# Prompt attention of a hybrid decoder layer: scores by halves of the sequence and classes of positions modulo 4, other load times for cache tiles, a later store

## The chip, the cores and the metric

The kernel runs on one core of one Trainium2 chip. The metric is the time of one execution on the device in microseconds (us); a kernel's time is the median of its runs. The engines have short names: PE multiplies matrices, DVE and ACT work on vectors, POOL is a slower vector engine, SP issues most DMAs. Each runs its own instruction stream in order and waits for the others through semaphores.

## What is computed

One layer of a decoder for two groups of tokens with the same weights: a prompt of 256 positions, and a sample group of 8 sequences with 4 new positions each, whose past keys and values lie in caches. Cut to what matters:

```
z = x @ w_in                       # h, gate_b, gate_c, q, k, v, g_a, g_b
A = gate_b * conv3(gate_c * h)     # causal, width 3; its last rows are a state to return
B: groups (window, dilation) = (128,1), (512,4), (2048,16), 4 heads of 128 each:
   position t sees s = t - dil*i, i = 0..128; score q.k*scale - slope*(t-s)
   softmax over the keys of all three groups together, per head
x1 = LN(ALPHA*x + W_o[sigmoid(g_a)*(A W_a) + sigmoid(g_b)*(B W_b)])
y  = LN(ALPHA*x1 + (silu(conv3(a))*b) W_down),  [a, b] = x1 W_up
```

Also returned are the new keys and values, the caches moved on, and the last rows of both convolutions. All is float32. In group 0 a position sees the 128 positions before it. In group 1 it sees only positions that are equal to it modulo 4, and in group 2 modulo 16; in a prompt of 256 all of those back to the start lie in the window.

## The kernel before, in words

*Products.* Everything is held as features by tokens: 128 partitions of features, 288 columns of tokens (256 of the prompt, 32 of the sample), the even tokens ahead of the odd ones in most tiles. A product (`product`, L202) multiplies one block of 128 output features with all tokens: up to 16 blocks of 128 input features, each with three matmuls (L221, L222, L223), high part of the weight by high and low part of x, and low part of the weight by high part of x. ACT makes the high part of a weight block (`whi`) and DVE the low part (`wlo`) from the float32 load, both in `split` (L227), in two halves of 8 blocks. `prepare` (L177) issues the load of the next product's weights on SP (L182), 1 MB each, into one of three buffers `wst`; the halves of `whi` and `wlo` have four buffers each. The products come in this order: 12 for the queries, 24 for keys and values (head by head), 48 for mixer A, 32 for gate a beside W_a, 32 for gate b beside W_b, 16 for W_o, and the feed-forward part.

*Order.* A scheduler places the instructions on each engine when the kernel is built, from the order in which the code emits them and its own guess of times. `behind` (L139) ties a DMA to stand behind the last weight load. So the place of an instruction on its engine is fixed, and an engine whose next instruction waits does nothing else.

*Prompt attention* (`prompt_attention`, L344) is a generator for one head, advanced between products. First the scores: the queries of the even positions and those of the odd positions (`qb` 0 and 1), 128 each, against 256 keys in group 0 (L353) and against the 128 keys of the same parity in groups 1 and 2 (L355); distances `m_dist`, with 1e30 at keys that aren't seen, are multiplied and added on DVE (L364). Row maximum (L369), exponential on ACT (L371), and normalisation (L373) follow. Two products later PE transposes the values (L378) and the weights (L387), and ACT copies them to SBUF (L384, L391). One product later PE multiplies them (L395). These matmuls are float32, and each is two instructions on PE; a transpose is one.

*Distances* are loaded by `load_distances` (L328) with four DMAs, L336 and L337, after the fifth query product.

*The sample's part.* The caches of groups 0, 1 and 2 come as 18 key tiles (`in_ck`) and 18 value tiles (`in_cv`) of 1 MB, through three buffers `cache`. Tiles 0 and 1 belong to group 0 and are multiplied on PE (L472). Each other tile is multiplied elementwise, half on ACT (L437) and half on DVE (L441), and summed on DVE (L443). `sample_events` (L449) gives each step a place, counted in products: a key tile n at 13, 14, then 2.75 apart; value tiles at 64, 65, then 2.5 apart; its load (`cache_load`, L423, issued at L425) 5 products ahead (L551).

*The state of mixer A*, `cm`, is filled by POOL (L620, L621) and stored at L657, after the 48 products of mixer A.

*Copies* of the caches from input to output (L146) go on SP behind some of the weight loads from the 93rd on.

Of the kernel before, what the change touches and what calls it, by code (L numbers as in the profile page):

```python
# [35 lines left out]
NG, NH = 3, 4  # L36
DIL = (1, 4, 16)
BAND = 128
SCALE = P**-0.5
# [15 lines left out]
C_M0 = C_TM + NT  # L55
# [3 lines left out]
C_M1 = C_M0 + NG * P  # L59
# [17 lines left out]
SQ = 32  # L77
SCORES_AT = 13
TILE_K = 2.75
VALUES_AT = 64  # L80
TILE_V = 2.5

# [11 lines left out]
def layer_kernel(ctx: ExitStack, tc: tile.TileContext, ins, outs):  # L94
    nc = tc.nc
    pe, dve, act, pool, sp = nc.tensor, nc.vector, nc.scalar, nc.gpsimd, nc.sync
# [12 lines left out]
    def sb(pl, shape, tag, dt=F32, bufs=None):  # L109
        return pl.tile(shape, dt, tag=tag, name=nm(tag), bufs=bufs)  # L110
# [22 lines left out]
    w_load = [None]  # L133
    steps_on = [False]
    n_product = [2]
# [3 lines left out]
    def behind(i, after):  # L139

        tc.add_manual_dep(i.ins, after.ins.name, no_sync, reason="pace")
# [156 lines left out]

    pa = sb(big, [P, KD * T], "yal")

    m_dist = pa[:, : 2 * NG * SEQ].rearrange("p (h g k) -> p h g k", h=2, g=NG)
    pa_at = [2 * NG * SEQ]

    def pa_take(n):
        pa_at[0] += n
        return pa[:, pa_at[0] - n : pa_at[0]]

    v_two = [pa_take(2 * NG * P).rearrange("p (b g d) -> p b g d", b=2, g=NG) for _ in range(2)]
    s_two = [pa_take(MW) for _ in range(2)]
    xs_flat = xs.rearrange("p k t -> p (k t)")  # L310
    q_all = xs_flat[:, : NH * NG * T].rearrange("p (j g t) -> p j g t", j=NH, g=NG)
    sT_two = [xs_flat[:, NH * NG * T + c * MW : NH * NG * T + (c + 1) * MW] for c in range(2)]
    oT = pa_take(2 * P)
    prm = sb(big, [P, R_W], "prm")
    ident = cst[:, C_ID : C_ID + P]
# [9 lines left out]
    )  # L325
    v_s = sb(big, [P, NH, NG, NS], "v_s")

    def load_distances():  # L328

        pool.memset(m_dist[: P // 2, :, :, P:], BIG)  # L330
        m0, m1 = (
            ins["cst"][:, c : c + NG * n * P].rearrange("(a h) (g k) -> h a g k", h=2, g=NG)
            for n, c in ((1, C_M0), (2, C_M1))
        )
        for h in range(2):
            behind(sp.dma_start(m_dist[: P // 2, h, :, :P], m0[h]), w_load[0])  # L336
            behind(sp.dma_start(m_dist[P // 2 :, h], m1[h]), w_load[0])  # L337

    def in_a_row(row):

        for before, i in zip(row, row[1:]):
            behind(i, before)

    def prompt_attention(j, qT, kT, vT):  # L344


        q4 = h3(qT)[:, :, :, :P]
        k4, v4 = (t[:, :, :SEQ].rearrange("p g (a h) -> p g h a", h=2) for t in (kT, vT))
        s3 = [att(MW) for _ in range(2)]
        row = [last_mm[0]]  # L350
        for qb in range(2):
            row += [
                pe.matmul(s3[qb][:, : 2 * P], q4[:, 0, qb], kT[:, 0, :SEQ], start=True, stop=True)  # L353
            ] + [
                pe.matmul(s3[qb][:, (1 + g) * P : (2 + g) * P], q4[:, g, qb], k4[:, g, qb], start=True, stop=True)  # L355
                for g in range(1, NG)
            ]
        in_a_row(row)
        s = s_two
        for qb in range(2):  # L360
            for g in range(NG):
                c, n = (0, 2 * P) if g == 0 else ((1 + g) * P, P)
                m = m_dist[:, qb, g] if g == 0 else t2(m_dist[:, qb, g])[:, qb]
                dve.scalar_tensor_tensor(  # L364
                    s[qb][:, c : c + n], m, -SLOPE[g][j] / SCALE, s3[qb][:, c : c + n], ALU.mult, ALU.add
                )
        for qb in range(2):
            st = sb(wk, [P, 4], "st", bufs=4)
            dve.reduce_max(st[:, 0:1], s[qb], AX.X)  # L369
            dve.tensor_scalar_mul(st[:, 1:2], st[:, 0:1], -SCALE)  # L370
            act.activation(s[qb], s[qb], AF.Exp, bias=st[:, 1:2], scale=SCALE, accum_out=st[:, 2:3])  # L371
            dve.reciprocal(st[:, 3:4], st[:, 2:3])
            dve.tensor_scalar_mul(s[qb], s[qb], st[:, 3:4])  # L373
        yield 2
        v = v_two[j % 2]
        pv = [att(NG * P) for _ in range(2)]
        row = [last_mm[0]] + [
            pe.transpose(  # L378
                pv[kb][:, g * P : (g + 1) * P], vT[:, 0, kb * P : (kb + 1) * P] if g == 0 else v4[:, g, kb], ident
            )  # L380
            for kb in range(2) for g in range(NG)
        ]
        for kb in range(2):
            act.copy(v[:, kb], pv[kb].rearrange("p (g d) -> p g d", g=NG))  # L384
        pt = [sb(ps, [P, MW], "acc") for _ in range(2)]
        in_a_row(row + [
            pe.transpose(pt[qb][:, c * P : (c + 1) * P], s[qb][:, c * P : (c + 1) * P], ident)  # L387
            for qb in range(2) for c in range(MW // P)
        ])
# [4 lines left out]
        in_a_row([last_mm[0]] + [  # L394
            pe.matmul(  # L395
                po[:, qb * P : (qb + 1) * P], v[:, c if c < 2 else qb, max(0, c - 1)], sT_two[qb][:, c * P : (c + 1) * P],
                start=c == 0, stop=c == MW // P - 1,
            )
            for qb in range(2) for c in range(MW // P)
        ])  # L400
        act.copy(oT, po)
        split(h2(ybh[:, j])[:, :, :P], h2(ybl[:, j])[:, :, :P], oT.rearrange("p (h a) -> p h a", h=2))


# [44 lines left out]
    def sample_events():  # L449
# [121 lines left out]
    for j in range(NH):  # L571
        for g in range(NG):
            act.copy(h2(q_all[:, j, g]), q_first.pop(0) if q_first else product(x))
            if j == 1 and g == 1:
                load_distances()
            elif j == 1:
                for dst, src in ((prm, ins["prm"]),) if g else (
                    (cst[:, :C_BM], ins["cst"][:, :C_BM]),
                    (bmask, ins["cst"][:, C_MASK : C_MASK + MASK]),
                ):  # L580
                    behind(sp.dma_start(dst, src), w_load[0])
            steps_on[0] = j * NG + g >= 4
        pool.tensor_copy(q_s[:, :, j, :].rearrange("p g (a h) -> p g h a", h=2), h3(q_all[:, j])[:, :, :, P:])
    for j in range(NH):
        kT, vT = (kv[:, j % 2, c] for c in range(2))
        for g in range(NG):
            for t in (kT, vT):
                act.copy(t[:, g, :].rearrange("p (a h) -> p a h", h=2), product(x).rearrange("p h a -> p a h"))
        pool.tensor_copy(k_s[:, :, j, :], kT[:, :, SEQ:])
# [49 lines left out]
    for i in range(KD):  # L639
# [14 lines left out]
        ya = sb(wk, [P, T], "ya", bufs=2)  # L654
        gated(ya, y, pb)
        split(yah[:, i], yal[:, i], ya)
    sp.dma_start(outs["o_cm"].rearrange("p (k r) -> p k r", k=KD), cm)  # L657


    ma = dd_all.rearrange("p (k t) -> p k t", t=T)  # L660
    for i in range(KD):
        pg = product(x)
        sg = sb(wk, [P, T], "h", bufs=2)
        act.activation(h2(sg), pg, AF.Sigmoid)
        o = product((h3(yah), h3(yal)))
        dve.tensor_tensor(h2(ma[:, i]), h2(sg), o, ALU.mult)
    n_product[0] += 1000
    for _ in steps:
        pass
# [388 lines left out]
```

## Time and profile before

| | us |
|---|---|
| median of 3 runs (1736.32 to 1737.24) | 1736.93 |
| the profiled execution | 1737.77 |
| its span, first to last instruction | 1736.0 |
| PE busy | 1714.2 |
| DVE busy | 1103.5 |
| ACT busy | 869.6 |
| POOL busy | 244.3 |
| SP's wait for DVE's split at L182 | 1310.8 |

The mean granted clock of PE is 0.996. A row of the order of time has the start in us, the length in us, engine, line, operation, output <- inputs, shapes and a count of equal ones that follow each other; in square brackets stands how long the engine was idle before it and what ended that. A row of a table of stretches has the stretch, its length, then busy time and count of instructions of PE, PEld (weight loads), DVE, ACT and POOL, then the granted clock, the DMA engines' share and GB/s. A row of waits has who waited for whom, then the total in us, the number of waits and the longest.

### The profile page before, as it was taken

How to read it: one execution, taken by the hardware profiler on the slowest of the kernel's cores; microseconds unless marked ns; L12 is line 12 of the kernel's file. 1: busy time of each engine (PE TensorE's matmuls, PEld its weight loads, DVE VectorE, ACT ScalarE, POOL GpSimd, SP SyncE). 2: the span in 40 equal slices, each digit the busy share in tenths (PEclk: the TensorE clock that was granted, in tenths of full speed). 3: DMA queues.
4: the chain of work that ended last, by engine and by line, in shares of the span. 5: the costliest groups of instructions: out<-in, count | busy, mean ns of one | idle time of the engine just before them, and what ended most of it. 6: DMA issues, size and time to landing. Idle time of an engine off the chain costs nothing.

```text
span 1736.0 us, 33482 instructions
## 1 busy us (share of the span) xinstructions
PE 1714.2 (99%) x14034; PEld 1708.0 (98%) x14034; DVE 1103.5 (64%) x1406; ACT 869.6 (50%) x1398; POOL 244.3 (14%) x404
## 2 busy tenths in 40 slices
PE   9999999999999999999999999999999999999996
PEld 9999999999999999999999999999999999999996
DVE  5576667657775564455788888865555554555554
ACT  5465555545555443344445655544444443344444
POOL 0000000000000000010354333200111100011165
PEclk9999999999999999999999999999999999999998
DMA  9676565665666676687866667666676666776652
GB/s 338 241 281 221 226 249 216 225 243 216 254 235 242 277 304 244 237 310 299 301 261 244 250 256 271 249 261 243 255 279 245 258 250 248 263 266 255 238 205 95
DMA packets 57463, 436.14 MB, mean 251 GB/s; under 512 B 7456, under 2 KB 9504, under 8 KB 17440
## 3 DMA queue, kind: packets, MB, share of 16 engines
q1 hardware_dynamic: 55584, 429.29, 65.3%
q10 hardware_dynamic: 1728, 4.72, 0.7%
q8 instruction: 109, 1.79, 0.4%
q14 instruction: 42, 0.34, 0.1%
HBM read 427.53 MB, written 94.53 MB: 301 GB/s over the span
## 4 chain that ended last, share of the span: by engine, by line
PE 92%; DMA 4%; DVE 2%; ACT 1%; issue 1%; SPq 0%; ACTq 0%; DVEq 0%
PE acc L221 30%; PE acc L223 30%; PE acc L222 30%; DMA cache<-in_cv 3%; PE acc L289 1%; DVE wlo L227 1%; DMA cache<-in_ck 1%; DVE sw L443 1%; PE att L395 0%; DMA wst<-in_w_in 0%; ACT cache L437 0%; ACT whi L227 0%; ACT yah L784 0%; DVE dd L760 0%; PE att L472 0%
## 5 line engine op out<-in xcount | busy, mean ns | idle before, releaser
L227 DVE TENSOR_TENSOR wlo<-wst,whi 128x1024 fp32r<-128x1024 f32 (+2 forms) x584 | 704.1, 1209 | 450.0 <-ACT whi L227 448.1
L227 ACT CAST whi<-wst 128x1024 fp32r<-128x1024 f32 (+2 forms) x584 | 590.9, 1016 | 705.4 <-PE acc L222 628.9
L221 PE MATMUL acc<-xh,whi 128*128 128x288 f32 (+1 forms) x3216 | 921.7, 287 | 0.3 <-ACT whi L227 0.3
L222 PE MATMUL acc<-xl,whi 128*128 128x288 f32 (+1 forms) x3216 | 919.2, 286 | 0.0
L223 PE MATMUL acc<-xh,wlo 128*128 128x288 f32 (+1 forms) x3216 | 917.0, 285 | 1.9 <-DVE wlo L227 1.9
L223 PEld LDWEIGHTS acc<-xh,wlo 128*128 128x128 f32 x3216 | 605.1, 188 | 2.8 <-DVE wlo L227 2.8
L221 PEld LDWEIGHTS acc<-xh,whi 128*128 128x128 f32 x3216 | 605.1, 188 | 1.5 <-issue 1.0
L222 PEld LDWEIGHTS acc<-xl,whi 128*128 128x128 f32 x3216 | 606.4, 189 | 0.0
L223 PE MATMUL acc<-yah,wlo 128*128 128x288 f32 x1216 | 348.3, 286 | 2.0 <-DVE wlo L227 1.9
L221 PE MATMUL acc<-yah,whi 128*128 128x288 f32 x1216 | 347.7, 286 | 0.2 <-ACT whi L227 0.2
L222 PE MATMUL acc<-yal,whi 128*128 128x288 f32 x1216 | 347.7, 286 | 0.0
L223 PEld LDWEIGHTS acc<-yah,wlo 128*128 128x128 f32 x1216 | 229.8, 189 | 3.0 <-DVE wlo L227 3.0
L221 PEld LDWEIGHTS acc<-yah,whi 128*128 128x128 f32 x1216 | 229.7, 189 | 0.4 <-ACT whi L227 0.4
L222 PEld LDWEIGHTS acc<-yal,whi 128*128 128x128 f32 x1216 | 229.8, 189 | 0.0
L620 POOL COPY qk_s<-u 128x2 f32<-128x2 f32 x44 | 38.0, 864 | 571.9 <-ACT u L835 449.0
L443 DVE TRANSPOSE_TENSOR_REDUCE sw<-cache 128x32 f32<-128x1024 f32 x64 | 77.3, 1232 | 0.4 <-ACT cache L437 0.3
L608 DVE SCALAR_TENSOR_TENSOR cy<-u,prm,cy 128x304 f32<-128x304 f32 x120 | 74.9, 624 | 3.8 <-ACT cy L606 0.7
L437 ACT ACTIVATE cache<-cache,dd 128x128 f32<-128x128 f32 x128 | 39.3, 388 | 58.3 <-DMA cache<-in_cv 58.3
L680 POOL TENSOR_TENSOR ya<-ya,dd 128x288 f32<-128x288 f32 x16 | 13.6, 850 | 296.3 <-DVE ya L679 296.3
L441 DVE TENSOR_TENSOR cache<-cache,dd 128x512 f32<-128x512 f32 x32 | 20.8, 688 | 52.3 <-DMA cache<-in_cv 52.3
L437 ACT ACTIVATE cache<-cache,qk_s 128x128 f32<-128x128 f32 x128 | 39.6, 389 | 22.5 <-DMA cache<-in_ck 21.4
L227 ACT CAST yah<-ya 128x288 fp32r<-128x288 f32 x76 | 32.7, 430 | 24.7 <-DVE ya L631 8.5
(181 smaller groups left out, 901.7 us busy)
## 6 DMA issues: line engine op xcount, KB each, us to landing
wst<-in_w_in SPq DMA_DIRECT2D x113, 1024.0 KB, 4.9
wst<-in_w_up SPq DMA_DIRECT2D x88, 1024.0 KB, 4.9
wst<-in_w_down SPq DMA_DIRECT2D x32, 1024.0 KB, 4.9
cache<-in_ck SPq DMA_DIRECT2D x18, 1024.0 KB, 7.2
cache<-in_cv SPq DMA_DIRECT2D x18, 1024.0 KB, 8.0
wst<-in_w_a SPq DMA_DIRECT2D x16, 1024.0 KB, 5.9
wst<-in_w_out SPq DMA_DIRECT2D x16, 1024.0 KB, 4.9
wst<-in_w_down SPq DMA_DIRECT2D x16, 768.0 KB, 4.2
```

The lines of the kernel that those rows point to most:

```text
L221: pe.matmul(out, hi[:, c, :], xh_k, start=k == 0, stop=False)
L222: pe.matmul(out, hi[:, c, :], xl_k, start=False, stop=False)
L223: last_mm[0] = pe.matmul(out, lo[:, c, :], xh_k, start=False, stop=k == nk - 1)
L227: return act.copy(hi, src), dve.tensor_tensor(lo, src, f32(hi), ALU.subtract)
L289: i = pe.matmul(o[b], first_w(term == 2, b, k), xk, start=k == 0 and term == 0, stop=k == KD - 1 and term == 2)
L437: act.activation(e_t, e_t, AF.Copy, scale=w[:, g + 1, j, b * NT + t : b * NT + t + 1])
L441: dve.tensor_tensor(e3, e3, w3, ALU.mult)
L443: dve.tensor_reduce(parts[:, g, :, j, b * NT : (b + 1) * NT].rearrange("p k j t -> p j t k"), c[:, 2 * half * cols : (2 * half + 2) * cols ...
L608: dve.scalar_tensor_tensor(y, u[:, i : i + YW], prm[:, w0 + i : w0 + i + 1], y, ALU.mult, ALU.add)
L620: pool.tensor_copy(dst[:, 0:2], u[:, SEQ : SEQ + 2])
L680: pool.tensor_tensor(m, m, ma[:, i], ALU.add)
```

## The change

The diff, cut to its core:

```
-MW = (2 + NG - 1) * P
+NM = NG * P
+NC = 4
+LEAD = 7
...
-    def load_distances():
-        pool.memset(m_dist[: P // 2, :, :, P:], BIG)
-        for h in range(2):
-            behind(sp.dma_start(m_dist[: P // 2, h, :, :P], m0[h]), w_load[0])
-            behind(sp.dma_start(m_dist[P // 2 :, h], m1[h]), w_load[0])
+    def distances():
+        pool.memset(s_two[0][:, P + 2 * SQ :], 0.0)
+        for b, c0 in ((1, C_M1), (0, C_M0)):
+            for c in range(NC):
+                for dst, m in (...):
+                    behind(sp.dma_start(dst, m), w_load[0])
+                    yield
...
+        for g in range(1, NG):
+            pool.tensor_copy(v_cls..., vT[:, g, :SEQ].rearrange("p (b u c) -> p c b u", b=2, c=NC))
...
-        for qb in range(2):
-            pe.matmul(s3[qb][:, : 2 * P], q4[:, 0, qb], kT[:, 0, :SEQ], ...)
-            pe.matmul(s3[qb][:, (1 + g) * P : (2 + g) * P], q4[:, g, qb], k4[:, g, qb], ...)  # g = 1, 2
+        for b in range(2):
+            n = (b + 1) * P
+            pe.matmul(s3[b][:, :n], q_0[:, b], kT[:, 0, :n], ...)
+            for g in range(1, NG):
+                for r in range(2):
+                    for c in range(2):
+                        at = slice(SQ * (2 * r + c), SQ * (2 * r + c + 1))
+                        pe.matmul(by_class[at, g - 1], q5[:, g, b, r, c], k5[:, r, c, : b + 1, g - 1], ...)
...
-        for qb in range(2) for c in range(MW // P): pe.transpose(pt[qb]...)
+        for b in range(2) for c in range(b + 2):    pe.transpose(pt[b]...)
...
-        for qb in range(2) for c in range(MW // P): pe.matmul(po[:, qb * P : (qb + 1) * P], v[...], sT_two[qb]...)
+        pe.matmul(h2(po), v[:, 0], sT_old, start=True, stop=False)
+        pe.matmul(po[:, P:], v[:, 1], sT_two[1][:, P : 2 * P], ...)
+        for c in range(NC):
+            pe.matmul(h2(po)[:, :, at], v[:, 2 + 2 * (c % 2) + c // 2], sT_cls[:, :, at], ...)
...
-                yield at - 5, partial(cache_load, which, n)
+                yield at - LEAD, partial(cache_load, which, n)
...
-            if j == 1 and g == 1:
-                load_distances()
+            if n_product[0] > 4:
+                for _ in range(3):
+                    next(m_loads, None)
...
+        for b in range(2):
+            pool.tensor_copy(q_0[:, b]..., h3(q_all[:, j])[:, 0, :, b * P // 2 : (b + 1) * P // 2]...)
...
-    sp.dma_start(outs["o_cm"]..., cm)              # after the 48 products of mixer A
+        if i == 1:                                 # two steps into gate a
+            sp.dma_start(outs["o_cm"]..., cm)
```

The rows of scores are now the first and the second half of the positions (b = 0 and 1), each ordered by class modulo 4. In group 0 the first half is multiplied with 128 keys only and the second with all 256. In groups 1 and 2 each class of 32 queries is multiplied with the 32 or 64 keys of its own class up to its half; the four classes write to four quarters of the partitions. Rows of weights are 192 and 384 long (the first padded to 256 with zeros for the transposes) in place of 512 each. Before the products of a head POOL copies group 0's queries into that order, and after them the values of groups 1 and 2 by class. The distances come with 16 DMAs, three after each query block from the sixth on. Cache tiles' loads are emitted 7 products ahead in place of 5. The store of mixer A's state is emitted two steps, four products, later.

More of the change, by code (lines that the diff above doesn't have):

```diff
@@ L344, in prompt_attention @@
     def prompt_attention(j, qT, kT, vT):
-        q4 = h3(qT)[:, :, :, :P]
-        k4, v4 = (t[:, :, :SEQ].rearrange("p g (a h) -> p g h a", h=2) for t in (kT, vT))
-        s3 = [att(MW) for _ in range(2)]
-        row = [last_mm[0]]
-        for qb in range(2):
[L352 to L357, printed above, removed]
@@ L358, in prompt_attention @@
-        in_a_row(row)
[L359 to L367, printed above, removed]
+        q5 = h3(qT)[:, :, :, :P].rearrange("p g r (b u c) -> p g b r c u", b=2, c=2)
@@ new lines, in prompt_attention @@
+        k5 = kT[:, 1:, :SEQ].rearrange("p g (b u c r) -> p r c b g u", b=2, c=2, r=2)
+        for g in range(1, NG):
+            pool.tensor_copy(
+                v_cls.rearrange("p c (b g u) -> p g c b u", b=2, g=2)[:, g - 1],
+                vT[:, g, :SEQ].rearrange("p (b u c) -> p c b u", b=2, c=NC),
+            )
+        s3 = [att((b + 1) * P + (b + 1) * 2 * SQ) for b in range(2)]
+        row = [last_mm[0]]
+        for b in range(2):
+            n = (b + 1) * P
+            row.append(pe.matmul(s3[b][:, :n], q_0[:, b], kT[:, 0, :n], start=True, stop=True))
+            by_class = s3[b][:, n:].rearrange("p (b g u) -> p g b u", g=2, u=SQ)
+            for g in range(1, NG):
+                for r in range(2):
+                    for c in range(2):
+                        at = slice(SQ * (2 * r + c), SQ * (2 * r + c + 1))
+                        row.append(pe.matmul(
+                            by_class[at, g - 1], q5[:, g, b, r, c], k5[:, r, c, : b + 1, g - 1], start=True, stop=True
+                        ))
@@ new lines, in prompt_attention @@
+        in_a_row(row)
+        s = [s_two[b][:, : (b + 1) * (P + 2 * SQ)] for b in range(2)]
+        for b in range(2):
+            n = (b + 1) * P
+            dve.scalar_tensor_tensor(
+                s[b][:, :n], m_dist[b][:, :n], -SLOPE[0][j] / SCALE, s3[b][:, :n], ALU.mult, ALU.add
+            )
+            dst, src = (t[:, n:].rearrange("p (b g u) -> p g b u", g=2, u=SQ) for t in (s[b], s3[b]))
+            for g in range(1, NG):
+                m = m_dist[b][:, g * n : (g + 1) * n].rearrange("p (b u c) -> p b u c", u=SQ, c=NC)[:, :, :, 0]
+                dve.scalar_tensor_tensor(dst[:, g - 1], m, -SLOPE[g][j] / SCALE, src[:, g - 1], ALU.mult, ALU.add)
@@ L376, in prompt_attention @@
         pv = [att(NG * P) for _ in range(2)]
[L377 to L385, printed above, removed]
+        row = [last_mm[0]]
+        for n in range(2 * NG):
+            out = pv[n // NG][:, n % NG * P : (n % NG + 1) * P]
+            src = vT[:, 0, n * P : (n + 1) * P] if n < 2 else v_cls[:, n - 2]
+            row.append(pe.transpose(out, src, ident))
+        for n in range(2):
+            act.copy(v[:, n * NG : (n + 1) * NG], pv[n].rearrange("p (b d) -> p b d", d=P))
+        pt = [sb(ps, [P, (b + 2) * P], "acc") for b in range(2)]
         in_a_row(row + [
-            pe.transpose(pt[qb][:, c * P : (c + 1) * P], s[qb][:, c * P : (c + 1) * P], ident)
-            for qb in range(2) for c in range(MW // P)
+            pe.transpose(pt[b][:, c * P : (c + 1) * P], s_two[b][:, c * P : (c + 1) * P], ident)
+            for b in range(2) for c in range(b + 2)
         ])
@@ L393, in prompt_attention @@
         po = att(2 * P)
[L394 to L401, printed above, removed]
+        row = [last_mm[0]]
+        row.append(pe.matmul(h2(po), v[:, 0], sT_old, start=True, stop=False))
+        row.append(pe.matmul(po[:, P:], v[:, 1], sT_two[1][:, P : 2 * P], start=False, stop=False))
+        for c in range(NC):
+            at = slice(c * SQ, (c + 1) * SQ)
+            row.append(pe.matmul(
+                h2(po)[:, :, at], v[:, 2 + 2 * (c % 2) + c // 2], sT_cls[:, :, at], start=False, stop=c == NC - 1
+            ))
+        in_a_row(row)
+        o_b = oT.rearrange("p (r b u c) -> p b r c u", r=2, b=2, c=2)
+        for b in range(2):
+            act.copy(o_b[:, b], po[:, b * P : (b + 1) * P].rearrange("p (r c u) -> p r c u", r=2, c=2))
         split(h2(ybh[:, j])[:, :, :P], h2(ybl[:, j])[:, :, :P], oT.rearrange("p (h a) -> p h a", h=2))
@@ L585, in layer_kernel @@
         kT, vT = (kv[:, j % 2, c] for c in range(2))
+        for b in range(2):
+            pool.tensor_copy(
+                q_0[:, b].rearrange("p (r c u) -> p r c u", r=2, c=2),
+                h3(q_all[:, j])[:, 0, :, b * P // 2 : (b + 1) * P // 2].rearrange("p r (u c) -> p r c u", c=2),
+            )
         for g in range(NG):
@@ L666, in layer_kernel @@
         dve.tensor_tensor(h2(ma[:, i]), h2(sg), o, ALU.mult)
+        if i == 1:
+            sp.dma_start(outs["o_cm"].rearrange("p (k r) -> p k r", k=KD), cm)
     n_product[0] += 1000
```

32 lines of the change are left out of this document (18 added, 14 removed).

## Prediction

> **What bounds the kernel now.** I read the page's busy times first, then the table of stretches, then the waits of PE, then the order of time on PE, DVE and SP.
>
> ```profile
> span 1736.0 us, 33482 instructions
> PE 1714.2 (99%) x14034; PEld 1708.0 (98%) x14034; DVE 1103.5 (64%) x1406; ACT 869.6 (50%) x1398; POOL 244.3 (14%) x404
> ...
> 430.00:530.00 100.00, 100.00 (x818) 100.00 (x817) 72.17 (x95) 54.35 (x102) 5.04 (x20) 1.00 0.65 253
> 533.00:633.00 100.00, 95.59 (x758) 93.28 (x757) 63.28 (x70) 51.38 (x92) 0.24 (x2) 1.00 0.67 263
> ```
>
> PE is busy from end to end at a granted clock of 1.00, so the time is what PE is given to do plus what it loses. In 430 to 530 it starts 818 instructions in 100 us, 122.2 ns each, so one product of 48 matmuls takes 5.87 us. In 533 to 633 it starts only 758: 60 × 122.2 ns = 7.3 us are lost there. PE waits in that stretch for DVE's weight splits, and DVE waits for cache tiles:
>
> ```profile
> PE acc L223 <- DVE wlo L227: 3.7, 6, 1.2
> ...
> DVE cache L441 <- DMA cache<-in_cv: 32.4, 6, 6.4
> ```
>
> The view of waits counts 3.7 us of it for PE; the rest is restart after each wait. So two things can move the end: PE's work in the prompt attention, and these 7.3 us.
>
> **Prompt attention, on PE's path.** One head stands in three blocks between products (order of time, PE; start, length, name, count of instructions; a float32 matmul is two instructions, a transpose is one):
>
> ```profile
> 115.41 0.59 PE L353 MATMUL att<-dd,yah 128*128 128x256 f32 x2
> 115.84 0.61 PE L355 MATMUL att<-dd,yah 128*128 128x128 f32 x4
> 116.30 0.59 PE L353 MATMUL att<-dd,yah 128*128 128x256 f32 x2
> 116.73 0.62 PE L355 MATMUL att<-dd,yah 128*128 128x128 f32 x4
> 117.10 0.37 PE L221 MATMUL acc<-xh,whi 128*128 128x288 f32 x1
> ...
> 128.97 0.86 PE L378 MATMUL att<-cst,dd 128*128 128x128 f32 x6
> 129.66 1.04 PE L387 MATMUL acc<-cst,yal 128*128 128x128 f32 x8
> 130.45 0.37 PE L221 MATMUL acc<-xh,whi 128*128 128x288 f32 x1
> ...
> 136.43 1.95 PE L395 MATMUL att<-yah,yal 128*128 128x128 f32 x16
> 138.13 0.37 PE L221 MATMUL acc<-xh,whi 128*128 128x288 f32 x1
> ```
>
> From start to start: scores 1.69, transposes 1.48, outputs 1.70 us. The new shapes, 32 stationary columns in four places of the array, exist in the sample's part:
>
> ```profile
> 83.43 0.28 PE L223 MATMUL acc<-xh,wlo 128*128 128x288 f32 x1
> 83.64 1.08 PE L472 MATMUL att<-cache,sw 128*32 128x128 f32 x32
> 84.65 0.39 PE L221 MATMUL acc<-xh,whi 128*128 128x288 f32 x1
> ...
> 378.02 0.28 PE L223 MATMUL acc<-xh,wlo 128*128 128x288 f32 x1
> 378.23 0.40 PE L493 MATMUL att<-qk_s 128*32 128x32 f32 x24
> 378.56 1.97 PE L502 MATMUL att<-squares,sw 128*128 128x32 f32 x16
> 380.36 0.37 PE L221 MATMUL acc<-xh,whi 128*128 128x288 f32 x1
> ```
>
> With 128 moving columns one costs 1.01 / 32 = 32 ns, with 32 columns 0.33 / 24 = 14 ns, and going into such a block costs 0.21 - 0.12 = 0.09 us. Neither row has 64 columns; between them by columns lies 20 ns (bounds 14 and 32).
>
> Scores after: group 0 of the first half, two instructions as half of a row of L355, 0.21; 16 small ones of 32 columns, 0.09 + 16 × 0.014 = 0.31; group 0 of the second half as L353, 0.43; 16 of 64 columns, 0.09 + 16 × 0.020 = 0.41. Sum 1.36, saves 0.33. Transposes: 11 in place of 14; three of L387 at 0.79 / 8 go, saves 0.30. Outputs: 12 instructions in place of 16: two of 256 columns 0.43, two of 128 at 1.70 / 16 make 0.21, eight with a full stationary and 64 columns as L502, 1.80 / 16 = 0.11 each, 0.90. Sum 1.54, saves 0.16. Per head 0.79, **four heads 3.1 us**. Bounds: small ones at 32 and 32 ns, 0.5 us per head less; at 14 and 14, 0.1 more: 1.1 to 3.5 us.
>
> The third head also waits:
>
> ```profile
> 209.91 0.85 PE L378 MATMUL att<-cst,dd 128*128 128x128 f32 x6
> 211.26 1.09 PE L387 MATMUL acc<-cst,yal 128*128 128x128 f32 x8 [0.50 <-DVE yal L373]
> 212.11 0.37 PE L221 MATMUL acc<-xh,whi 128*128 128x288 f32 x1
> ```
>
> 2.20 us against 1.48: **0.7 us**. In the built order of before, DVE and ACT do a cache tile between the third and fourth heads' row maxima and exponentials; in that of the changed kernel no tile stands inside a softmax of these two heads. I take the 0.7 as gone; if another head waits instead, it stays. What is next late there is nothing: the next block has two products, 11.7 us, ahead of it.
>
> Beside PE: DVE, ACT have smaller tiles per head, POOL gets four copies per head more (queries of group 0, values by class).
>
> ```profile
> L589 POOL COPY qk_s<-dd 128x96 f32<-128x96 f32 x4 | 3.4, 838 | 134.9 <-ACT dd L588 134.9
> ```
>
> At the 838 ns for 96 elements of L589, two copies of 256 are 4.5 us against the 11.9 us between 117.10 and the transposes at 128.97 that need them: hidden; without that cover each head would wait 4.5 us. The queries' copies have the head's six products before them.
>
> **Distances: 16 loads on SP in place of 4.** They stand between the weight loads 4 to 9, 3 to a product. An issue takes 0.3 to 0.6 us of SP. ACT's casts show whether weights are late there (waits, 27 to 75 us):
>
> ```profile
> ACT whi L227 <- PE acc L222: 20.4, 14, 1.9
> ```
>
> The casts wait for PE to free buffers, so loads are early; 1.5 us of SP per product is hidden. Taken as 0; if not, about 1 us.
>
> **States stored later.** In both built orders the store of the mixer states stands on SP right behind weight load 84 and ahead of load 85.
>
> ```profile
> 532.64 0.35 SPq L657 DMA_DIRECT2D out_o_cm<-cm  x1
> 534.61 0.33 SPq L182 DMA_DIRECT2D wst<-in_w_a  x1
> 534.99 0.42 SPq L425 DMA_DIRECT2D cache<-in_cv  x1
> ...
> 533.40 1.18 DVE L227 TENSOR_TENSOR wlo<-wst,whi 128x1024 fp32r<-128x1024 f32 x1
> ```
>
> After the store, load 85 still waits for the split that ends at 533.40 + 1.18 = 534.58, which frees its buffer. The store holds up nothing, and moving it frees nothing: 0.
>
> **Cache tiles seven products ahead.** In the built orders each value tile's load does come two weight loads earlier (in before behind loads 68, 70, 73, 75, ... 98; in the changed kernel behind 66, 68, 71, 73, ... 96). But DVE's use of the tile has moved forward with it: in both it stands just ahead of a half split of the weight load before, or of that load's first half. So DVE still reaches the tile before it lands:
>
> ```profile
> 538.69 1.23 DVE L227 TENSOR_TENSOR wlo<-wst,whi 128x1024 fp32r<-128x1024 f32 x1
> 543.30 1.29 DVE L441 TENSOR_TENSOR cache<-cache,dd 128x512 f32<-128x512 f32 x2 [3.38 <-DMA cache<-in_cv]
> 544.61 2.42 DVE L443 TRANSPOSE_TENSOR_REDUCE sw<-cache 128x32 f32<-128x1024 f32 x2
> 546.95 1.18 DVE L227 TENSOR_TENSOR wlo<-wst,whi 128x1024 fp32r<-128x1024 f32 x1
> ```
>
> That is a loop: a split frees a buffer, SP issues a weight load and the tile (534.99), the tile lands 8.3 us later, DVE multiplies and reduces it, and only then splits the weight that lets SP go on (548.13): 13.5 us for two loads that PE uses in 11.7. Its pace over many loads, from SP's issues of loads 75, 90 and 100 (load 85 is the 534.61 above), and PE's need of load 72's second half, whose split released load 75:
>
> ```profile
> 471.31 0.33 SPq L182 DMA_DIRECT2D wst<-in_w_in  x1
> 567.01 0.33 SPq L182 DMA_DIRECT2D wst<-in_w_in  x1
> 629.38 0.33 SPq L182 DMA_DIRECT2D wst<-in_w_in  x1
> ...
> 475.50 0.29 PE L223 MATMUL acc<-xh,wlo 128*128 128x288 f32 x1
> ```
>
> 158.07 / 25 = 6.32 us per load against 5.87: 25 loads fall 11.3 us behind. The split was 4.2 us ahead (475.50 - 471.31) at the start; 11.3 - 4.2 = 7.1, which is the 7.3 lost. In the changed kernel the paced stretch is also 25 loads (73 to 98), two loads earlier. What differs is the lead with which it begins. Three tiles come together behind loads 65 and 66 where two did, one tile's work (1.29 + 2.42 = 3.7 us) more ahead of load 65's split. From there I carry the loop's own terms forward: an estimate of 1.9 us of lead at load 70, where before had 4.2 at 72. So 11.3 - 1.9 = 9.4 us lost in place of 7.3: **+2.1 us**. Bounds: no tile waits left (-7.3), and the worst five loads' pace with no lead (+11, below). The key tiles come 2.75 products apart, 16.1 us, which covers a loop of 13.5: 0.
>
> **Sum.** -3.1 - 0.7 + 2.1 = -1.7. The profiled execution took 1737.77 us (span 1736.0 and 1.8 around it), 0.84 above the median 1736.93: 1736.1 for its like, **1735.2** for the median.
>
> **Rivals.**
>
> *The longer lead is one.* If tiles land before DVE reaches them, the 7.3 us go as well: 1736.93 - 3.8 - 7.3 = 1725.8; with half, 1729.5. For it: DVE's 32.4 us of waiting are what PE's loss hangs on. Against it: DVE's built order. 0.22.
>
> *The loop starts without lead (slower).* Place: DVE's split of load 65, behind three tiles. If it ends after PE's need and the gap isn't closed by load 69, all 30 loads from 66 to 96 run in the loop; at the pace of loads 85 to 90, (567.01 - 534.61) / 5 = 6.48, they lose 30 × 0.61 = 18.3 us, 11.0 more than now: 1736.93 - 3.8 + 11.0 = 1744.1. It turns slower than before at a pace over 6.24 (11.1 us lost). For it: 3.7 us more work there. Against it: three loads without a tile follow. 0.15.
>
> *The stride costs.* Keys of a class lie 16 bytes apart where they lay 8 apart (every fourth element for every second). If the small scores then stream at half pace, 16 × 14 + 16 × 20 ns = 0.54 us per head are added, 2.2 in all: 1737.4. No row of before has that stride. [...] Chance of the rival: 0.13.
>
> *Forecast*, "seven ahead" gives no longer lead: 0.50, own range 1732.0 to 1738.5.
>
> **Chances.** 0.2% is 3.5 us, about what a measurement can tell from no change: faster is below 1733.5, slower above 1740.4. Forecast 0.12 faster, 0.36 same, 0.02 slower; long lead 0.22 faster; stride 0.13 same; no lead 0.13 slower, 0.02 same. Faster 0.34, same 0.51, slower 0.15. The range 1729.0 to 1741.0 leaves out half of the long lead (0.11) and most of the no-lead case (0.1).
>
> **What would show it.** Score blocks near 1.4 us (2.0 if the stride costs), transposes 1.2, outputs 1.5; no gap before the third head's second transposes. Stretches of 100 us between 440 and 620 that start fewer than 818 instructions: with the forecast the first gap comes near load 77, some five products earlier than now, and about 75 instructions are missing in all; with a real lead none are, and DVE's wait for value tiles falls below 20 us; with no lead gaps begin at about 434 us. The forecast is wrong if a tile's landing changes by more than 1 us, or if the small matmuls don't run four at a time.

## The result, and the profile after

| | before | after |
|---|---|---|
| median, us (15 runs each on one chip) | 1737.24 | 1733.28 |
| lowest and highest, us | 1734.69, 1738.57 | 1732.10, 1735.76 |
| span of the profiled execution, us | 1736.0 | 1732.5 |

The ratio is 0.9977, 95% interval 0.9970 to 0.9984: 4.0 us faster, where 1.7 were forecast. The forecast of the time, 1735.2, was 1.9 us too high. Two of its three terms were far off, and they were off in opposite directions.

The page of the kernel after, its busy times, and then its table of stretches:

```profile
span 1732.5 us, 33671 instructions
PE 1712.0 (99%) x14102; PEld 1703.6 (98%) x14102; DVE 1100.5 (64%) x1406; ACT 866.8 (50%) x1402; POOL 259.3 (15%) x420
```

```profile
433.00:533.00 100.00, 99.31 (x809) 99.10 (x809) 71.55 (x96) 53.05 (x103) 8.79 (x22) 1.00 0.64 251
533.00:633.00 100.00, 96.90 (x779) 95.64 (x779) 64.61 (x70) 51.59 (x87) 0.24 (x2) 1.00 0.69 276
```

A full stretch starts 818. From 433 to 533 us 9 are now missing where before had 817, and from 533 to 633 us 39 where before lacked 60. I use this count throughout as **the gaps at the tiles**: 48 × 122.2 ns = 5.9 us, before 61, 7.5 us. (Added up from the starts of the product matmuls between 430 and 660 us, what exceeds 122 ns is 5.7 and 7.3.) DVE's wait for value tiles from 430 to 660 us, in the view of waits (52.0 in the kernel before):

```profile
DVE cache L464 <- DMA cache<-in_cv: 48.5, 12, 6.1
```

The first gap is where the prediction put it, at load 77, but the loop then lost less: 48 instructions are missing where about 75 were forecast. Order of time on PE:

```profile
503.13 0.28 PE L224 MATMUL acc<-xl,whi 128*128 128x288 f32 x1
504.10 0.39 PE L225 MATMUL acc<-xh,wlo 128*128 128x288 f32 x1 [0.69 <-DVE wlo L229]
```

One head on PE in the kernel after, same view:

```profile
115.97 0.38 PE L367 MATMUL att<-dd,yal 128*128 128x128 f32 x2
116.28 0.43 PE L373 MATMUL att<-dd,yah 128*32 128x32 f32 x16
116.64 0.70 PE L367 MATMUL att<-dd,yal 128*128 128x256 f32 x2
117.27 0.66 PE L373 MATMUL att<-dd,yah 128*32 128x64 f32 x16
117.86 0.39 PE L223 MATMUL acc<-xh,whi 128*128 128x288 f32 x1
...
129.74 0.38 PE L401 MATMUL att<-cst,dd 128*128 128x128 f32 x2
...
130.86 0.37 PE L223 MATMUL acc<-xh,whi 128*128 128x288 f32 x1
...
136.83 0.59 PE L414 MATMUL att<-yah,yal 128*128 128x256 f32 x2
...
138.30 0.37 PE L223 MATMUL acc<-xh,whi 128*128 128x288 f32 x1
...
209.91 0.38 PE L401 MATMUL att<-cst,dd 128*128 128x128 f32 x2
...
211.03 0.37 PE L223 MATMUL acc<-xh,whi 128*128 128x288 f32 x1
```

Scores 1.89 us (before 1.69, forecast 1.36), transposes 1.12 (1.48, 1.18), outputs 1.47 (1.70, 1.54): 4.48 against 4.87, 0.4 us per head where 0.79 was forecast. The third head's transposes now take 1.12 us like the others, so its wait of 0.7 is gone.

The difference of the spans, 3.5 us, is then: four heads 1.6, the third head's wait 0.7, gaps at the tiles 1.6, and 0.6 lost at the start of the run, 3.3 in all; 0.1 more lies behind the last product. The start is scatter: the first head begins at 115.97 in place of 115.41, and in the other profiled executions, e6 to e8 with their instructions added at the start left out, between 115.59 and 116.23, so the one of before was the earliest.

### The profile page after: what moved, and what is told of

The parts are those of the page before. It is cut to its first block, busy times and chain, and to the rows that moved or that the text cites. A ratio compares the mean times of both kernels' runs of the same rounds, so it can differ in the third digit from the quotient of the medians.

```text
span 1732.5 us, 33671 instructions
## 1 busy us (share of the span) xinstructions
PE 1712.0 (99%) x14102; PEld 1703.6 (98%) x14102; DVE 1100.5 (64%) x1406; ACT 866.8 (50%) x1402; POOL 259.3 (15%) x420
## 4 chain that ended last, share of the span: by engine, by line
PE 90%; DMA 5%; DVE 3%; issue 1%; ACT 1%; SPq 0%; ACTq 0%; DVEq 0%
PE acc L223 29%; PE acc L225 29%; PE acc L224 29%; DMA cache<-in_cv 4%; DVE wlo L229 1%; PE acc L291 1%; DVE sw L466 1%; DMA dd<-in_w_in 0%; DVE cache L464 0%; ACT yah L812 0%; PE att L495 0%; DVE dd L788 0%; ACT cache L460 0%; PE att L373 0%; PE att L367 0%
## 5 line engine op out<-in xcount | busy, mean ns | idle before, releaser
L464 DVE TENSOR_TENSOR cache<-cache,dd 128x512 f32<-128x512 f32 x32 | 20.7, 686 | 48.5 <-DMA cache<-in_cv 48.5
```

What stands on the lines that cost most here:

```text
L464: dve.tensor_tensor(e3, e3, w3, ALU.mult)
```

## The experiments

My theory at the outset was the prediction's *loop*: DVE reaches a tile before it lands, and the split queued behind it is late. Rivals: the seven products are a real lead; the tiles have nothing to do with it. For the attention: *stride* (keys 16 bytes apart) or *switch* (going in and out of the 32-row places). In each group of four experiments the kernel before ran on the same chip: medians 1738.49 (e1 to e4), 1738.07 (e5 to e8), 1737.90 (e9 to e12). Times between groups are compared by their ratios to it.

### e1: the kernel after with five products ahead

```
-LEAD = 7
+LEAD = 5
```

> The kernel after with the cache tiles loaded five products ahead again; attention and store stay as changed. Its built order on DVE in the value tiles' stretch is that of the kernel before. Theory 'loop' (the tile's use on DVE moves with its load, PE loses by the loop of load, tile, split): PE's gaps between 430 and 640 us add up to about 7 us as before (7.3), in place of the 5.5 of the kernel after; the time is 1.7 us over the kernel after, about 1735.0. Rival 'heads only' (the seven products change nothing, the two profiled runs differ by scatter of the landings): gaps of 5.5 to 7.3 at random, time within 0.5 us of the kernel after.

Measured: 1732.41, ratio 0.9957 (0.9944 to 0.9971). By the ratios it is 3.5 us faster than the whole change, with intervals that only just touch, and not slower. Its five runs fall into two groups, 1732.41 to 1732.91 and 1728.38 to 1728.77; the profiled one is of the first.

```profile
433.00:533.00 100.00, 98.43 (x786) 98.00 (x785) 72.23 (x96) 54.65 (x105) 7.41 (x22) 0.98 0.62 239
533.00:633.00 100.00, 100.00 (x818) 100.00 (x817) 68.32 (x74) 53.48 (x93) 0.24 (x2) 1.00 0.74 290
```

32 instructions are missing, 3.9 us, all before 533 us; after that there is no gap, though DVE's order in that stretch is the one of the kernel before. Only 2.1 us of the 3.9 are a wait for a split behind a tile, at 485 to 488 us. The other 1.7 are a lower clock: from 488.3 us on, right behind that wait, the granted clock was 0.50 for 3.4 us, which is the mean of 0.98 in the row. A wait as long in e4 (1.5 us at 503) had no such stretch behind it, and why this one had is open. Both expectations missed. The order on DVE alone doesn't settle what the loop loses.

### e2: the kernel before with seven products ahead

```
-                yield at - 5, partial(cache_load, which, n)
+                yield at - 7, partial(cache_load, which, n)
```

> The kernel before with the cache tiles loaded seven products ahead; attention and store as before. 'Loop' with the phase of the kernel after: PE's gaps in the value tiles' stretch 5.5 us in place of 7.3, so 1.7 us under the kernel before. 'Heads only': no difference, within 0.5 us. The prediction's own term said 2.1 us over the kernel before.

Measured: 1731.68, ratio 0.9962 (0.9949 to 0.9974), 6.8 us under the kernel before, four times what was expected.

```profile
433.00:533.00 100.00, 100.00 (x818) 100.00 (x817) 77.71 (x102) 57.48 (x106) 4.53 (x22) 1.00 0.67 254
533.00:633.00 100.00, 99.99 (x816) 99.77 (x815) 63.51 (x68) 50.79 (x85) 0.24 (x2) 1.00 0.75 295
```

Two instructions are missing. Its third head's transposes, order of time:

```profile
210.44 0.85 PE L378 MATMUL att<-cst,dd 128*128 128x128 f32 x6
211.14 1.04 PE L387 MATMUL acc<-cst,yal 128*128 128x128 f32 x8
211.93 0.37 PE L221 MATMUL acc<-xh,whi 128*128 128x288 f32 x1
```

1.49 us: with the tile order of "seven ahead" the 0.7 is gone under the old attention too. So each half of the change alone gives about 6 to 7 us, and both together 4. Two effects that don't add up ask for something that both shift.

**What both shift.** I laid the landings of the value tiles beside the packets of the DMA queues. Two queues carry instructions: in the page of the kernel after "q8 instruction: 110, 1.80" and "q14 instruction: 42, 0.34" (packets, MB). PE and its weight loads have 2 × 14102 instructions; 1.80 MB over that is 64 bytes each, so I take q8 for PE's code, 256 instructions per packet of 16 KB (1.80 MB / 110). At 61.1 ns per instruction (two per 122.2 ns) that is one packet per 15.6 us; 58 were counted in the 900 us from 700 to 1600 of the kernel before, with single distances from 10 to 20 us. A tile comes every 2.5 products, 14.7 us. Two tiles of the kernel after; transfers and queues from the tile's issue on, first tile 31, then tile 32 (counted from 0 over keys and values):

```profile
q1 hardware_dynamic: 286, 2.11, 88.7%
q8 instruction: 1, 0.02, 1.0%
...
cache<-in_cv SPq DMA_DIRECT2D x1, 1024.0 KB, 8.3
```

```profile
q1 hardware_dynamic: 275, 2.11, 87.8%
...
cache<-in_cv SPq DMA_DIRECT2D x1, 1024.0 KB, 6.9
```

With a packet in its transfer the tile lands after 8.3 us, without one after 6.9. Landing of tiles 24 to 32 in us, worked out from the transfers of all profiled executions; a star marks a packet of PE's code between -0.1 and +6 us of the tile's issue:

```
tile                 24   25   26   27   28   29   30   31   32   gaps, us
before              6.9  7.3* 8.6* 8.0* 6.9  8.8* 8.3* 8.3* 8.2*   7.5
after               7.7  7.5  8.0* 8.3* 8.2* 8.4* 8.2* 8.3* 6.9    5.9
e1                  8.4* 8.6* 8.3* 7.0  6.8  7.4  6.9  6.9  7.0    3.9
e2                  7.0  6.9  7.0  6.9  6.9  7.6* 8.5* 7.3* 6.9    0.2
e6 (below)          7.3  7.0  6.9  7.1  6.9  6.9  7.0  6.9  7.1    0.1
e7 (below)          6.9  7.2* 7.4* 8.3* 8.3* 8.0* 8.4* 8.6* 8.3*   7.2
```

Of e1's 3.9 us, 1.7 are the lower clock told above. Over all 14 kernels 49 of these tiles were hit, 8.2 us on average (7.0 to 8.9), and 77 were not, 7.0 (6.8 to 7.7). The new theory, *fetch*: the loop loses where packets of PE's code fall into the tiles' transfers, over several tiles running, since the two periods differ by only 1 us; where they fall depends on how many PE instructions come ahead (the attention adds 136, 8.3 us) and on when the tiles are loaded (two products, 11.7 us).

### e3: the keys of a class beside each other

```
-  k5 = kT[:, 1:, :SEQ].rearrange("p g (b u c r) -> p r c b g u", b=2, c=2, r=2)
+  k5 = kT[:, 1:, :SEQ].rearrange("p g (r c b u) -> p r c b g u", b=2, c=2, r=2)
```

> The kernel after with the keys of a class read from neighbouring elements in place of every fourth, so the scores of groups 1 and 2 use other keys than asked for; sizes and counts stay. 'Stride': the four small matmuls beside each other took 54 to 61 ns for 32 columns and 104 to 118 ns for 64 in the kernel after, while the sample's (neighbouring elements) took 32 for 32 and 127 for 128; so here 32 and 64, 0.3 us less per head, score block 1.6 us in place of 1.89, 1.2 us less in all. 'No stride' (the pace comes from something else, as the row offsets or the weight loads): block stays at 1.89, time unchanged.

Measured: 1732.27, ratio 0.9967 (0.9954 to 0.9979).

```profile
116.00 0.38 PE L367 MATMUL att<-dd,yal 128*128 128x128 f32 x2
116.32 0.34 PE L373 MATMUL att<-dd,yah 128*32 128x32 f32 x16
116.58 0.70 PE L367 MATMUL att<-dd,yal 128*128 128x256 f32 x2
117.21 0.43 PE L373 MATMUL att<-dd,yah 128*32 128x64 f32 x16
117.58 0.39 PE L223 MATMUL acc<-xh,whi 128*128 128x288 f32 x1
```

The block takes 1.58 us in place of 1.89: *stride* holds. Four beside each other take 55 ns for 64 columns where the kernel after has 104 to 118, and 31 for 32 where it has 54 to 61. The pair of group 0 still takes 0.63. Its own gaps at the tiles were 5.3 us (43 missing), of which 1.7 are again 3.4 us at a granted clock of 0.50, from 535.2 us on, behind a wait; so the time shows only about what the block gives.

### e4: group 0 first, one block of small ones

```
         for b in range(2):
             n = (b + 1) * P
             row.append(pe.matmul(s3[b][:, :n], q_0[:, b], kT[:, 0, :n], ...))
+        for b in range(2):
+            n = (b + 1) * P
             by_class = ...
```

> The kernel after with both score matmuls of group 0 first and all 32 small ones behind them, so PE goes into the 32-row places once per head and out of them once. 'Switch' (each way in or out costs about 0.1 us and more): group 0's second pair takes 0.43 in place of 0.63 us and the first small block's way out (0.17 at its last instruction in place of 0.06) goes: 0.3 us less per head, block 1.6 us, 1.2 us less in all. 'No switch' (the 320 and 309 ns of the second pair are the price of its 256 columns from the copied queries): block 1.8 to 1.9, time unchanged.

Measured: 1732.76, ratio 0.9971 (0.9961 to 0.9980).

```profile
115.82 0.81 PE L367 MATMUL att<-dd,yal 128*128 128x128 f32 x4
116.57 0.91 PE L375 MATMUL att<-dd,yah 128*32 128x32 f32 x32
117.41 0.39 PE L223 MATMUL acc<-xh,whi 128*128 128x288 f32 x1
```

1.59 us in place of 1.89: *switch* holds too. The pass into the small places and out again that this order saves cost about 0.3 us. This run's gaps were 6.7 us (55 missing), 0.8 more than in the kernel after: a gain of 1.2 us can't be read from the time while the gaps vary by as much.

### e5: the tiles' multiplications behind their load's split

```
+        own = n_split[tile_at[which, n] + BEHIND] if which == "cv" else None   # BEHIND = 0
...
+                    behind(i, own[0])    # ACT's multiplication behind the cast
+                    behind(i, own[1])    # DVE's behind the subtraction
```

> The kernel after, in which DVE's and ACT's multiplications of a value tile are put behind the split of the weight load that stands right ahead of the tile's load; nothing else changes. In the kernel after they stood ahead of it. 'Loop' (PE's losses between 430 and 660 us come from splits queued behind a tile that hasn't landed): the tile then has about three products, 17 us, for a landing of 7 to 8.5; DVE waits for no value tile, PE's gaps there fall from 5.7 to under 0.5 us, and the time is some 5 us under the kernel after, about 1729.5 on this chip. Rival 'something else' (DMA or DVE has no room in that stretch): gaps stay at 3 to 7 us, named after another releaser.

Measured: 1728.93, ratio 0.9946 (0.9934 to 0.9959).

```profile
433.00:533.00 100.00, 100.00 (x817) 100.00 (x817) 78.20 (x104) 57.84 (x109) 11.11 (x24) 1.00 0.69 251
533.00:633.00 100.00, 100.00 (x818) 100.00 (x818) 64.44 (x66) 51.58 (x87) 0.00 (x0) 1.00 0.76 284
```

No gap is left, and DVE's wait for value tiles, 48.5 us in the kernel after, is in no row any more. Two of the tiles 24 to 32 were still hit (8.4 and 8.1 us), and it cost nothing. *Loop* holds as the way in which a late tile reaches PE. DVE, order of time:

```profile
530.97 1.23 DVE L233 TENSOR_TENSOR wlo<-wst,whi 128x1024 fp32r<-128x1024 f32 x1 [0.48 <-ACT whi L233]
532.12 1.29 DVE L472 TENSOR_TENSOR cache<-cache,dd 128x512 f32<-128x512 f32 x2
533.32 2.37 DVE L476 TRANSPOSE_TENSOR_REDUCE sw<-cache 128x32 f32<-128x1024 f32 x2
```

The multiplication has no wait in brackets.

### e6 and e7: the kernel before with 128 and 256 PE instructions more at the start

```
-    for _ in range(N_WARM):
+    for _ in range(N_WARM - 2):            # e7: - 4
         pe.matmul(o, zero[:, :P], zero, ...)
+    for n in range(33):                    # e7: 66
+        pe.matmul(o[n % 4 * SQ : (n % 4 + 1) * SQ, :SQ], f32(zero)[:, :SQ], f32(zero)[:, :SQ], ...)
```

> The kernel before with 33 small float32 matmuls of 32 x 32 zeros in place of two of the 18 idle matmuls ahead of the first product: 128 PE instructions more ahead of all others, and nothing else. Theory 'fetch': PE's instructions come in packets of 16 KB, one per 15.7 us (256 instructions of 64 bytes), each 0.9 to 1.0 us on one DMA engine; a value tile (one per 14.7 us) whose transfer such a packet falls into lands in 8.2 to 8.8 us, the others in 6.9. Tiles 26 to 32 of the kernel before were hit. 128 instructions put the packets half a period, 7.8 us, aside: tiles 25 to 31 land in about 7 us, hits come from tile 33 on, PE's gaps between 430 and 660 us fall from 7.3 to 0 to 2 us, and the time falls by 5 to 7 us against the kernel before. Rival 'no fetch' (the landings scatter for other reasons): within 1 us of the kernel before.

> The same with 66 small matmuls in place of four idle ones: 256 PE instructions more, one whole packet. 'Fetch': the packets fall where they fell in the kernel before, tiles 26 to 32 are hit again, PE's gaps are 6 to 9 us and the time within 1 us of the kernel before. Rival 'the small matmuls help in another way': the time falls as with 128 or more.

Measured: e6 1730.70, ratio 0.9959 (0.9945 to 0.9972), 7.4 us faster; e7 1739.16, ratio 1.0012 (1.0003 to 1.0021), 1.1 us slower. The runs of e7 scatter from 1738.20 to 1743.77, more than those of any other kernel here; the profiled one is the fastest of them, and what the others lose is open. The stretches of e6, then of e7:

```profile
433.00:533.00 100.00, 100.00 (x817) 100.00 (x816) 76.29 (x101) 57.27 (x106) 6.61 (x22) 1.00 0.65 248
533.00:633.00 100.00, 100.00 (x818) 100.00 (x817) 65.88 (x71) 53.47 (x93) 0.24 (x2) 1.00 0.78 303
```

```profile
433.00:533.00 100.00, 100.00 (x817) 100.00 (x816) 73.80 (x97) 55.83 (x105) 4.46 (x22) 1.00 0.64 247
533.00:633.00 100.00, 95.51 (x760) 93.37 (x758) 62.53 (x69) 50.62 (x92) 0.24 (x2) 1.00 0.68 261
```

Half a packet of idle work over 400 us earlier removes the gaps, and a whole packet brings them back, which also bears out the 256 instructions per packet. *Fetch* holds: the programs differ in nothing but the idle matmuls at the start, and e6's order on DVE is that of the kernel before from end to end. Tile 30 in both, from its issue on (e6, then e7):

```profile
q1 hardware_dynamic: 266, 2.05, 85.7%
...
cache<-in_cv SPq DMA_DIRECT2D x1, 1024.0 KB, 7.0
```

```profile
q1 hardware_dynamic: 267, 2.05, 85.9%
q8 instruction: 1, 0.02, 1.8%
...
cache<-in_cv SPq DMA_DIRECT2D x1, 1024.0 KB, 8.4
```

### e8: the same 128 on the kernel after

> The kernel after with 128 PE instructions more ahead of the first product, as above. 'Fetch': tiles 26 to 31, which were hit 3 to 6 us after their issue, land in about 7 us; hits move to tiles 32 to 35; PE's gaps fall from 5.7 to 0 to 2 us, the time by 3 to 5 us to 1730 on this chip. 'No fetch': unchanged within 1 us.

Measured: 1729.26, ratio 0.9951 (0.9938 to 0.9963): close to e5, with no instruction missing (817 and 818). Tiles 26 to 30 landed in 6.8 to 7.6 us; hits came at 31, 33 and 34, and no gap followed. Its order on DVE is that of the kernel after from end to end. So before, e1, e6 and e7 share one order in this stretch, and after, e2 and e8 the other, and with either order the gaps come and go with the packets.

### e9: order, neighbouring keys and one block together

To e4's and e5's edits this adds real copies of the keys:

```
+            pool.tensor_copy(
+                k_cls[g - 1].rearrange("p n (b u) -> p n b u", b=2),
+                kT[:, g, :SEQ].rearrange("p (b u n) -> p n b u", b=2, n=NC),
+            )
...
-    by_class[at, g - 1], q5[:, g, b, r, c], k5[:, r, c, : b + 1, g - 1], ...
+    by_class[at, g - 1], q5[:, g, b, r, c], k_cls[g - 1][:, 2 * c + r, : (b + 1) * SQ], ...
```

> Three edits together on the kernel after: the tiles' multiplications behind their load's split (as in the run before), the keys of groups 1 and 2 copied by POOL into class order so that the small matmuls read neighbouring elements, and both score matmuls of group 0 ahead of all small ones. Theory (stride, switch and order add up): score block 1.57 + 1.59 - 1.88 = 1.28 us where the kernel after has 1.88, 0.6 us less per head, 2.4 in all; no gaps between 430 and 660 us; time 2.4 us under the run with the order alone, 1726.5 where that gave 1728.9. Rival (the copies of the keys come late: two copies of 256 elements ahead of the scores, 2 to 4 us of POOL beside one product of 5.9): PE waits at each score block, 1728 or more.

Measured: 1727.02, ratio 0.9936 (0.9924 to 0.9949), the fastest here.

```profile
115.59 0.82 PE L376 MATMUL att<-dd,yal 128*128 128x128 f32 x4
...
116.83 0.39 PE L227 MATMUL acc<-xh,whi 128*128 128x288 f32 x1
```

The score block takes 1.24 us (expected 1.28), 0.65 under the kernel after, and PE doesn't wait ahead of it. The time is 0.5 over what was expected of it. The intervals of e5 and e9 overlap, but e11 and e12 below have e5's order and ran in e9's group: e9 is 1.9 and 2.0 us under them, and 2.3 and 2.4 in the medians of the spans (1724.8 against 1727.1 and 1727.2), which is what was expected. The 0.4 between the two is time outside the span, 2.2 us in e9 and 1.8 in the others; no run shows where it comes from.

### e10: order and seven products on the kernel before

The edits of e2 and e5, attention and store as before.

> The kernel before with tiles loaded seven products ahead and their multiplications behind their load's split: attention and store as before. With no gap at the tiles on either side, its distance to the changed kernel with the same order is the attention (and the store) alone. By the blocks in the traces (4.87 against 4.47 us per head) 1.6 us over that run: 1730.5 where it gave 1728.9. By the prediction's 0.79 per head it would be 3.1: 1732.0. Rival 'attention gives nothing': equal.

Measured: 1730.54, ratio 0.9958 (0.9945 to 0.9972), no instruction missing. e11 and e12, with the new attention and in the same group, are 1.6 and 1.5 us under it; e5, of another group, is 2.1 under it by the ratios. The attention is worth about 1.6 us to the time, as its rows say, not 3.1.

### e11 and e12: five products ahead, and the store at its old place, both with e5's order

```
-LEAD = 7            # e11
+LEAD = 5
...
+    sp.dma_start(outs["o_cm"].rearrange("p (k r) -> p k r", k=KD), cm)     # e12, ahead of the gates
     ma = dd_all.rearrange("p (k t) -> p k t", t=T)
```

> The kernel after with tiles loaded five products ahead and their multiplications behind their load's split. Theory (the number of products ahead isn't what counts once DVE's use stands behind the split): equal to the run with seven, within 0.5 us, no gaps of PE at the tiles. Rival (seven are needed for the landing): gaps, 1 to 5 us slower.

> The kernel after with the tiles' multiplications behind their load's split and the store of the mixer states back at its old place in the program, ahead of the output gates. Theory (the store holds up nothing): equal to the run with the store moved, within 0.5 us. Rival (the store on SP delays a weight load): a gap of PE at the products of the first gates, 0.3 us or more slower.

Measured: 1728.93, ratio 0.9949 (0.9937 to 0.9962), and 1729.01, ratio 0.9948 (0.9935 to 0.9960): both equal to e5. Once DVE's use stands behind the split, five products ahead serve as well as seven, and the store's place gives nothing.

## Why the prediction was right or wrong

*The time* lay in the forecast's own range, 1.9 us under its centre, by luck, because errors cancelled: the heads with the third head's wait gave 2.3 us where 3.8 were forecast, the start took 0.6, and the tiles gave 1.6 where 2.1 were to be lost. By the prediction's own line, 1733.5, the result is just on the faster side, to which its mechanism gave 0.12 and all its cases together 0.34.

*Heads, -3.1: right in mechanism, half in size* (-1.6, e10). Transposes and outputs came out 0.06 and 0.07 us better than forecast. The term that failed is the score block, 1.36 forecast and 1.89 measured, and it failed in two parts of about the same size. First, the switch: I charged 0.09 us for each way in and nothing for the way out; group 0's pair between the two small blocks takes 0.63 us where it took 0.43 before. One pass in and out cost 0.3 us (e4). Second, the stride: the rival "the stride costs" was true, at 0.3 us per head (e3) where I had priced 0.54. No run of before shows the half pace that the 0.54 assumed. e3 shows it: four small matmuls of 64 columns beside each other take 55 ns with neighbouring keys and took 104 to 118 with every fourth element, those of 32 columns 31 and 54 to 61; but that starts from 14 and 8 ns per small matmul, where I had 20 and 14. The bounds of the prediction, 14 to 32 ns per small matmul, held the 64-column ones (26 to 30 ns each); what they left out was the switch.

*Third head's wait, -0.7: right*, but neither the attention nor the tiles' order is needed for it. e2, with the old attention and the new order, has no wait there, and e6, with the attention and the order of before, has none either (1.49 us). What counts is when the key tile lands that DVE takes inside this head's softmax: 9.2 us after its issue in the kernel before, with a packet of PE's code 5.8 us behind that issue and 2.5 us of DVE waiting, and 8.1 in e6, without a packet and without a wait of DVE. The new order takes the tile out of that place, as the prediction said.

*Copies on POOL, distances on SP: right*, no wait stands at either. *Store, 0: right* (e12).

*Cache tiles, +2.1: wrong, with the wrong sign* (-1.6). That DVE's use moves with the load, that this makes a loop, and that the first gap comes near load 77 was right (503.13; e5 cuts the loop and the gaps go). The step that failed is "from there I carry the loop's own terms forward": I took the pace of 6.32 us per load as a property of the loop, from one profiled execution. It is a property of where PE's code packets fall, as e6 shows: the same order, and no gap. The tiles of before were hit from 25 to 32 but for one, those of after from 26 to 31, and the loop of after went from the split of load 70 (459.02) to that of load 95 (614.71) at 155.69 / 25 = 6.23. So 25 loads fell 9.0 us behind in place of 11.3, and with 3.0 us of lead in place of 1.9 that is 6.0 lost in place of 9.4. The rows for it were in the profile of before: landings of 6.9 and 8.3 us in the same stretch, of which the prediction quotes 8.3 alone. Its own sign of being wrong, a tile's landing that changes by more than 1 us, came true: tile 28 went from 6.9 to 8.2 and tile 32 from 8.2 to 6.9.

*The rival "the longer lead is real"* fell as a mechanism: DVE still waited 48.5 us for value tiles in the kernel after, and e11 has five products and no gap. That seven ahead alone gave 6.8 us on the kernel before (e2) is by the same theory the shift of the tiles against the packets, 11.7 us of 15.6. The attention's 136 instructions bring the packets 8.3 us earlier, and the two products bring the tiles 11.7 us earlier, so together the packets lie only 3.4 us later against the tiles, and little of either gain is left. The traces fit this: the packet came 5.1, 3.3 and 4.5 us behind the issue of tiles 26 to 28 in the kernel after, and -0.1, 1.1 and -0.5 us in the kernel before. e6 to e8 show the effect of such a shift; that the two shifts alone make the 5.9 us of the kernel after is argued, not shown by itself. *The rival "no lead"* didn't come: load 70 had 3.0 us of lead (its split ended at 459.02, and PE needed it at 462.02) where I had estimated 1.9.

## What to carry to other kernels

Where two changes that each help don't help together, or a loss wanders between variants of a kernel, look for something periodic that both shift; here padding PE's stream by half a code packet and by a whole one told it. An instruction that may wait for data belongs, in its engine's order, behind the work that mustn't wait for it: putting the tiles' use behind the split (ratio 0.9946 in e5) gave more than any choice of how early to load (0.9977 with seven products ahead, 0.9957 with five in e1). Small matmuls beside each other paid for each entry and exit (0.3 us a pass here) and for moving elements that weren't neighbours (0.3 us a head), so gather them into one block and their elements beside each other.

## What was not expected of the hardware

What I take for PE's code comes as DMA packets beside the data all through the run: 110 of 16 KB in the kernel after, 58 in the 900 us from 700 to 1600 of the kernel before, about one in 15.6 us. Over all runs half of them took up to 0.96 us, the shortest 0.88 and the longest 2.1. A value tile of 1 MB into whose load one fell landed after 8.2 us on average, the others after 7.0. The trace doesn't tell which of the 16 engines carried the packet, so how it holds up the load is not shown. Behind two waits of PE (e1, e3) the granted clock was 0.50 for 3.4 us; no run shows what brings that on.
